# Squares summed after a trip through DRAM, scales spread as rows, and one pair of attention heads taken earlier

## The chip, the cores and the metric

The kernel runs on one core of a Trainium2 chip. The metric is the device time of one execution in microseconds (us). Instruction durations come from the hardware profile of one execution. The five engines each run their own instruction stream in order: PE (matrix multiplies and the transposes made with them), DVE (vector), ACT (scalar), POOL (GpSimd) and SP, which here only issues DMA transfers.

## The reference, cut to what matters

The program is one decoder layer on 512 tokens with 2048 channels. The part that the change touches is the normalisation of queries and keys (per head of 64 channels), the norm of the input, and the LayerNorm of the convolution branch:

```python
h = _rms_norm(x, norm1_g[l])
proj = h @ w_in[l]
aq, ak, av, bu, bg, cq, ck, cv = jnp.split(proj, splits, axis=-1)
aq = _rms_norm(aq.reshape(B, S, A_HEADS, HEAD_DIM), a_q_g[l])
ak = _rms_norm(ak.reshape(B, S, A_HEADS, HEAD_DIM), a_k_g[l])
out_a = _dilated_mixture(aq, ak, av).reshape(B, S, A_WIDTH)
out_b = _conformer_conv(bu, bg, conv_w[l], conv_b[l], conv_ln_g[l], conv_ln_b[l])
cq = _rms_norm(cq.reshape(B, S, C_Q_HEADS, HEAD_DIM), c_q_g[l])
ck = _rms_norm(ck.reshape(B, S, C_KV_HEADS, HEAD_DIM), c_k_g[l])
out_c, _ = _band_attention(cq, ck, cv, C_WINDOW - 1, sinks=c_sinks[l])
mix = jnp.concatenate([out_a, out_b, out_c], axis=-1)
x = x + mix @ w_out[l]
h2 = _rms_norm(x, norm2_g[l])
x = x + (jax.nn.silu(h2 @ w_gate[l]) * (h2 @ w_up[l])) @ w_down[l]
```

`_rms_norm` divides by the root of the mean square over the last axis; A has 8 query heads and three dilated patterns, C has 16 query heads on 2 key heads, B is a gated convolution with 31 taps and a LayerNorm over 512 channels.

## The kernel before, in words

Activations lie with channels on the 128 partitions and the 512 tokens along the row. The input projection is 30 column tiles of 128 channels, taken in the order of the table `PROJ`: value tiles first, then the convolution's (`bu`, `bg`), then C's key tile `ck`, C's eight query tiles `cq0` to `cq7`, and A's key and query tiles `ak0` to `ak3`, `aq0` to `aq3`. A tile holds two heads of 64 channels. Each tile is 16 steps of three matmuls (`mm3`, L318 to L321: the high part of the weights by the high and the low part of the activations, and the low part by the high one), 48 in all.

The output projection follows in two halves. Each takes eight rows of mixed channels in the order of `ROWS`: the first half the eight C rows, the second the A and B rows. After it comes the feed-forward part, from some 605 us to the end, which the change does not touch.

What stands where in each engine's stream is written by hand. A calendar (`Ticks`) is advanced one tick after each six matmuls of an input projection (eight ticks for a tile) and after each twelve of the output projection, and `ticks.after(n, fn)` has `fn` issue its instructions n ticks on. Nothing is measured at run time: a function issues at its tick, and if its data is late, its engine waits there with all that stands behind it.

At the end of a projected query or key tile, `head_scales` (L568) makes the scale of each token and head. ACT copies the tile out of PSUM (`raw`, L571); SQ = 3 ticks later PE transposes the four 128x128 blocks into a PSUM bank (`flip`, L576), so that tokens lie on partitions; ACT squares them (L581); DVE sums each head's 64 squares (a reduce of 128x512 and an addition, L586 to L588); POOL raises the 8 sums of each partition to the power -1/2 (L593). For a query tile (`do_q`) the raw values are also cast into a high part (L609, ACT) and a low part (L614, DVE), and four SP transfers copy halves of them into place (L616, L617). The query's scale is applied later, inside the exponentials of its attention. `"q at"` and `"k at"` are the ticks from which attention heads may use a tile.

For a key tile (`do_k`) the scales must lie along the row, beside the raw values: ACT widens the 8 columns to 512 (`widen`, L630), PE transposes that in four blocks (L637), DVE multiplies (L643), SP copies the halves into the other 64 partitions (L649), ACT and DVE make the high and low parts (L655, L660). The input norm's scale `r1` and the LayerNorm's scale `lrs` are spread in the same way by `spread` (L372), four transposes each (L376). The LayerNorm's scale then multiplies the four convolution tiles `y` on DVE (L560), ACT applies SiLU (L562), and the tiles become rows b0 to b3 of the second half.

The convolution's taps (L521) are 120 DVE instructions set between all of this up to 412 us. The weights of the projections are loaded by SP (L265), cast by ACT (`wh`, L297 and L277) and split by DVE (`wl`, L301 and L278). The attention of a head pair issues scores, exponentials (ACT, L811, with POOL's normalisation L822), transposes on PE (L855) and the weighing of values on PE (L879 and L880, with low parts `a2pl` made on DVE, L866).

Of the kernel before, what the change touches and what calls it, by code (L numbers as in the profile page):

```python
# [15 lines left out]
P = 128  # L16
T = 512
# [24 lines left out]

C_TICKS = (1, 6, 2, 2, 2, 2, 4, 1, 5)
# [4 lines left out]
        "bg2 cq2 cq7 ak2 cq4 cq6 bu3 bg3 ak0 aq0 ak1 aq1 aq2 ak3 aq3").split()  # L48
ROWS = "c0 c3 c1 c5 c2 c7 c4 c6 a0 a1 b2 b1 b0 b3 a2 a3".split()
# [80 lines left out]
def kernel(ctx: ExitStack, tc: tile.TileContext, xT, wi, wo, wgu, wd, cst_in, outT):  # L130
# [241 lines left out]
    def spread(src4, name, b=None):  # L372

        b = bank(name) if b is None else b
        for i in range(NT):
            nc.tensor.transpose(b[:, i * P:(i + 1) * P], src4[:, i:i + 1].to_broadcast([P, P]), ident)  # L376
        return b

# [117 lines left out]

    def spread_r1():
        b = spread(r1, "r1s")
        nc.scalar.copy(r1b, b)
# [57 lines left out]
    def ln_out(mix):  # L557
        b = spread(ln["r"], "lrs")
        for j in range(NB):
            nc.vector.tensor_mul(yconv[j], yconv[j], b)  # L560
        for j in range(NB):
            nc.scalar.activation(yconv[j], yconv[j], AF.Silu, bias=col(C_LB + j), scale=col(C_LG + j))  # L562
            mix[f"b{j}"] = yconv[j]
        for n, name in enumerate(r for r in ROWS if r[0] == "b"):
            ticks.after(1 + n, split_mix, name)


    def head_scales(b, name, then):  # L568
# [10 lines left out]
        def square(b2):  # L579
            sq = slot(name + "sq")  # L580
            nc.scalar.activation(sq, b2, AF.Square)  # L581
            ticks.after(1, total, sq)

        def total(sq):
            v = cp.tile([P, NT, 2], F32, name=name + "v", tag="hsv", bufs=3)
            nc.vector.tensor_reduce(v.rearrange("p a b -> p (a b)"), sq.rearrange("p (a b) -> p a b", b=HD),  # L586
                                    axis=mybir.AxisListType.X, op=ALU.add)
            nc.vector.tensor_add(v, v, c64[:, :, None].to_broadcast([P, NT, 2]))  # L588
            ticks.after(1, power, v)
# [6 lines left out]
        ticks.after(SQ, flip)  # L596
        return raw

    def do_q(box, b, name):
# [3 lines left out]
        raw = head_scales(b, name, then)  # L603
        box["q at"] = ticks.now + SQ + 4
# [15 lines left out]
    def do_k(box, b, name, gi):  # L620
        def then(r):
            ticks.after(KW, widen, r)

        raw = head_scales(b, name, then)
        box["k at"] = ticks.now + SQ + KW + TD + 10
        both = []

# [1114 lines left out]
```

## Time and profile before

| | before |
|---|---|
| median of 3 runs | 1852.05 us (1851.46 to 1852.13) |
| the profiled execution | 1851.51 us |
| its span in the trace | 1849.7 us |
| time around the span | 1.8 us |
| granted PE clock over the span | 1.000 of full speed |
| PE busy, instructions | 1844.3 us, 8548 |
| POOL busy, instructions | 1083.0 us, 681 |

The profiled execution lies 0.54 us under the median of the runs. A row of the trace's timeline gives start, duration, engine, line of the program, operation, output<-inputs, shapes and a count of merged equal instructions; durations of matmuls overlap, so the distance of two starts tells what one costs. A row of a line or tile view gives min/median/max in ns and the first and last start in us. A row of the waits gives the total, the number and the longest of the waits of one kind.

### The profile page before, as it was taken

What the parts mean: (1) busy time and instruction counts of PE and PEld (TensorE: products, weight loads), DVE (VectorE), ACT (ScalarE), POOL (GpSimd) and SP (SyncE); (2) the same over time, 40 slices, a digit from 0 to 9 for tenths busy, and PEclk for the clock granted to TensorE, in tenths of its full rate; (3) what the DMA queues carried; (4) which work ended last, traced back from release to release, by engine and by line L of the source; (5) the groups of instructions that cost most, each with busy time, mean ns of one, the idle gap of its engine ahead of it and who ended that gap; (6) DMA issues with size and microseconds to landing.
All of it is one profiled execution on the core that took longest, in us unless ns stands there. A gap on an engine that the chain in (4) does not pass through costs nothing.

```text
span 1849.7 us, 26751 instructions
## 1 busy us (share of the span) xinstructions
PE 1844.3 (100%) x8548; PEld 1538.4 (83%) x8548; DVE 1533.8 (83%) x2318; ACT 1370.2 (74%) x1956; POOL 1083.0 (59%) x681
## 2 busy tenths in 40 slices
PE   9999999999999999999999999999999999999999
PEld 7888888888888888888888888888888888888888
DVE  7688899997589888898888888888888677779887
ACT  6235555554466788889988889898898987777775
POOL 5013444462153568666685666857667777766786
PEclk9999999999999999999999999999999999999999
DMA  7334333443387459788787887788879786488984
GB/s 263 130 105 115 102 103 95 123 120 120 103 293 272 129 177 295 219 264 272 230 278 227 280 264 234 261 246 264 279 240 371 230 298 222 164 281 284 306 234 125
DMA packets 318556, 398.50 MB, mean 215 GB/s; under 512 B 80976, under 2 KB 210128, under 8 KB 318416
## 3 DMA queue, kind: packets, MB, share of 16 engines
q1 hardware_dynamic: 318272, 396.79, 66.9%
q8 instruction: 68, 1.11, 0.2%
q14 instruction: 72, 0.59, 0.1%
q10 hardware_dynamic: 144, 0.01, 0.0%
HBM read 308.90 MB, written 80.22 MB: 210 GB/s over the span
## 4 chain that ended last, share of the span: by engine, by line
PE 99%; ACT 0%; DVE 0%; DMA 0%; issue 0%; SPq 0%; ACTq 0%; DVEq 0%
PE out L1391 62%; PE out L1283 6%; PE o L321 3%; PE o L319 3%; PE o L320 3%; PE cq L319 2%; PE cq L320 2%; PE cq L321 2%; PE in L320 1%; PE aq L319 1%; PE ak L319 1%; PE ak L321 1%; PE aq L321 1%; PE bu L320 1%; PE ak L320 1%; PE bu L321 1%
## 5 line engine op out<-in xcount | busy, mean ns | idle before, releaser
L1391 PE MATMUL out<-wh,h 128*128 128x512 f32 x2464 | 609.0, 389 | 0.1
L1391 PEld LDWEIGHTS out<-wh,h 128*128 128x128 f32 x2464 | 462.3, 188 | 96.7 <-issue 0.5
L1391 PE MATMUL out<-wl,h 128*128 128x512 f32 x1232 | 329.3, 389 | 0.0
L1391 PEld LDWEIGHTS out<-wl,h 128*128 128x128 f32 x1232 | 231.2, 188 | 48.1
L1391 PE MATMUL out<-wh,a 128*128 128x512 f32 x896 | 221.3, 389 | 0.0
L1391 PEld LDWEIGHTS out<-wh,a 128*128 128x128 f32 x896 | 168.2, 188 | 34.9
L1391 PE MATMUL out<-wl,a 128*128 128x512 f32 x448 | 119.7, 389 | 0.0
L1494 DVE TENSOR_TENSOR G<-G,out 128x512 f32<-128x512 f32 x132 | 83.9, 678 | 18.1 <-PE out L1391 18.1
L1391 PEld LDWEIGHTS out<-wl,a 128*128 128x128 f32 x448 | 84.1, 188 | 17.4
L521 DVE SCALAR_TENSOR_TENSOR y<-bu,cst,y 128x511 f32<-128x511 f32 (+14 forms) x120 | 94.5, 788 | 1.4
L277 ACT CAST wh<-w 128x1024 fp32r<-128x1024 f32 (+1 forms) x41 | 42.1, 1031 | 57.4 <-PE o L320 34.6
L1283 PE MATMUL out<-a,wh 128*128 128x512 f32 x330 | 80.1, 391 | 0.0
L297 ACT CAST wh<-w 128x1024 fp32r<-128x1024 f32 x52 | 54.8, 1054 | 32.3 <-PE bg L320 9.2
L301 DVE TENSOR_TENSOR wl<-w,wh 128x1024 fp32r<-128x1024 f32 x52 | 65.3, 1256 | 14.3 <-ACT wh L297 14.0
L1491 DVE TENSOR_TENSOR G<-G,out 128x512 f32<-128x512 f32 x110 | 68.5, 680 | 5.8 <-PE out L1391 5.8
L1283 PEld LDWEIGHTS out<-a,wh 128*128 128x128 f32 x330 | 60.2, 188 | 11.4
L1532 DVE STREAM_TRANSPOSE z<-s 128x256 f32<-128x256 f32 x88 | 60.1, 683 | 3.0
L278 DVE TENSOR_TENSOR wl<-w,wh 128x1024 fp32r<-128x1024 f32 (+1 forms) x41 | 51.7, 1262 | 9.1 <-ACT wh L277 8.9
L319 PE MATMUL o<-mh_c,wh 128*128 128x512 f32 x128 | 51.2, 400 | 0.0
L321 PE MATMUL o<-mh_c,wl 128*128 128x512 f32 x128 | 50.1, 391 | 0.0
L320 PE MATMUL o<-ml_c,wh 128*128 128x512 f32 x128 | 49.9, 390 | 0.0
L1436 DVE TENSOR_TENSOR Y<-Y,out 128x512 f32<-128x512 f32 x48 | 30.8, 685 | 17.6 <-PE out L1391 17.2
(2758 smaller groups left out, 5123.6 us busy)
## 6 DMA issues: line engine op xcount, KB each, us to landing
h<-hd SPq DMA_DIRECT2D x200, 256.0 KB, 5.8
od<-a SPq DMA_DIRECT2D x154, 256.0 KB, 6.6
a<-od SPq DMA_DIRECT2D x154, 256.0 KB, 6.0
w<-in_wi SPq DMA_DIRECT2D x59, 512.0 KB, 3.5
w<-in_wo SPq DMA_DIRECT2D x32, 512.0 KB, 3.4
hd<-h SPq DMA_DIRECT2D x56, 256.0 KB, 5.2
zd<-z SPq DMA_DIRECT2D x44, 256.0 KB, 4.9
x<-in_xT SPq DMA_DIRECT2D x16, 256.0 KB, 7.4
```

The lines of the kernel that those rows point to most:

```text
L278: eng.tensor_sub(lo[:, :n], t[:, :n], hi[:, :n].bitcast(F32))
L297: nc.scalar.copy(hi, t)
L301: nc.vector.tensor_sub(lo, t, hi.bitcast(F32))
L319: nc.tensor.matmul(out, wh, xh, start=start, stop=False)
L320: nc.tensor.matmul(out, wh, xl, start=False, stop=False)
L321: nc.tensor.matmul(out, wl, xh, start=False, stop=stop)
L521: nc.vector.scalar_tensor_tensor(yconv[j][:, i:], hconv[j][:, :T - i], c, yconv[j][:, i:], op0=ALU.mult, op1=ALU.add)
L1283: nc.tensor.matmul(out, lhs[:, s], rhs, start=begin, stop=last and low == flip[0] and x is xs[-1], skip_group_check=True)
L1391: nc.tensor.matmul(to[h], x[:, h * P:(h + 1) * P], v[:, j], start=sub == 0 and h not in started, stop=sub == 1 and n in (len(todo) - 1, le ...
L1491: op(t, t, b)
L1494: nc.vector.tensor_add(t, t, b)
L1532: nc.vector.transpose(to[:, :, h], s[:, cols].rearrange("p (c b) -> p b c", b=8))
```

## The change

The change has four parts.

1. All twelve query tiles and the key tile `ak2` are "folded". ACT squares the raw tile itself; SP writes the squares to DRAM and two ticks later fetches them back with four transfers, each of which puts 32 rows of four partitions' pieces side by side for one block of 128 tokens; four ticks later POOL adds the four pieces of each partition (a 128x256 and a 128x128 addition); three ticks later PE transposes one 128x128 block in place of four; DVE reduces 16 elements for each sum. From the end of a tile to its scale the calendar has 13 ticks (`FOLDED`) where it had 6.
2. Four scales are spread as rows (`all_rows`): those of the keys `ck` and `ak2`, the input norm's `r1` and the LayerNorm's `lrs`. PE makes one transpose, which gives 4 or 8 rows of 128; ACT copies them out, SP writes them to DRAM and reads them back repeated over the partitions. Before, there were four transposes each, and for keys the widening ahead of them.
3. The four multiplications by the LayerNorm's scale go from DVE to POOL.
4. In `PROJ`, `aq2` moves from behind `aq1` to ahead of `ak0`; in `ROWS`, the second half begins with a2 and a0 and ends with a1 and a3, where it began with a0 and a1 and ended with a2 and a3.

```diff
@@ -40,13 +40,19 @@
 SQ, KW, VD, TD, EV = 3, 4, 4, 2, 1
 
 
+ROW_KEYS = ("ck", "ak2")
+FOLD_AT = (2, 4, 3)
+FOLDED = 2 + sum(FOLD_AT) + 2
+ROWS_FROM, ROWS_AT, LN_ROWS_AT = 2, (1, 2, 3), (1, 1, 2)
+
+
 C_TICKS = (1, 6, 2, 2, 2, 2, 4, 1, 5)
 A_TICKS = (0, 7, 2, 1, 3, 1, 3, 1, 2)
 
 
 PROJ = ("av0 av1 av2 av3 bu0 bg0 bu1 bg1 cv ck cq0 cq3 cq1 cq5 bu2 "
-        "bg2 cq2 cq7 ak2 cq4 cq6 bu3 bg3 ak0 aq0 ak1 aq1 aq2 ak3 aq3").split()
-ROWS = "c0 c3 c1 c5 c2 c7 c4 c6 a0 a1 b2 b1 b0 b3 a2 a3".split()
+        "bg2 cq2 cq7 ak2 cq4 cq6 bu3 bg3 aq2 ak0 aq0 ak1 aq1 ak3 aq3").split()
+ROWS = "c0 c3 c1 c5 c2 c7 c4 c6 a2 a0 b2 b1 b0 b3 a1 a3".split()
 
 N_SLOTS = 68
 N_WIDE = 4
@@ -368,13 +374,6 @@
         rows = small(name + "s")
         nc.vector.tensor_reduce(rows, b.rearrange("p (a b) -> p a b", b=P), axis=mybir.AxisListType.X, op=ALU.add)
         return rows
-
-    def spread(src4, name, b=None):
-
-        b = bank(name) if b is None else b
-        for i in range(NT):
-            nc.tensor.transpose(b[:, i * P:(i + 1) * P], src4[:, i:i + 1].to_broadcast([P, P]), ident)
-        return b
 
     def small(name, cols=NT):
         return cp.tile([P, cols], F32, name=name, tag="small", bufs=24)
@@ -494,9 +493,30 @@
                     ticks.tick()
         return b
 
+    def all_rows(out, src, heads, name, waits, then, *args):
+
+        n = NT * heads
+        b = bank(name + "t")
+        nc.tensor.transpose(b[:n, :P], src, ident)
+        rows = cp.tile([2 * NT, P], F32, name=name + "w", tag="rows", bufs=2)
+        nc.scalar.copy(rows[:n], b[:n, :P])
+        d = tc.dram_tile([n, P], F32, name=name)
+
+        def put():
+            nc.sync.dma_start(d, rows[:n])
+            ticks.after(waits[1], back)
+
+        def back():
+            for h in range(heads):
+                part = out if heads == 1 else out[HALF[h]]
+                nc.sync.dma_start(part.rearrange("p (i c) -> p i c", i=NT),
+                                  bass.AP(tensor=d.tensor, offset=d.offset + h * P,
+                                          ap=[[0, P // heads], [heads * P, NT], [1, P]]))
+            ticks.after(waits[2], then, *args)
+        ticks.after(waits[0], put)
+
     def spread_r1():
-        b = spread(r1, "r1s")
-        nc.scalar.copy(r1b, b)
+        all_rows(r1b, r1, 1, "r1d", ROWS_AT, lambda: None)
 
 
     hconv, yconv = {}, {}
@@ -555,9 +575,12 @@
         ln["r"] = token_scale(ln.pop("s"), 512, "lv")[1]
 
     def ln_out(mix):
-        b = spread(ln["r"], "lrs")
+        b = slot("lrs")
+        all_rows(b, ln["r"], 1, "lrd", LN_ROWS_AT, ln_scale, mix, b)
+
+    def ln_scale(mix, b):
         for j in range(NB):
-            nc.vector.tensor_mul(yconv[j], yconv[j], b)
+            nc.gpsimd.tensor_mul(yconv[j], yconv[j], b)
         for j in range(NB):
             nc.scalar.activation(yconv[j], yconv[j], AF.Silu, bias=col(C_LB + j), scale=col(C_LG + j))
             mix[f"b{j}"] = yconv[j]
@@ -565,7 +588,7 @@
             ticks.after(1 + n, split_mix, name)
 
 
-    def head_scales(b, name, then):
+    def head_scales(b, name, folded, then):
 
         raw = slot(name + "raw")
         nc.scalar.copy(raw, b)
@@ -576,14 +599,36 @@
                 nc.tensor.transpose(b2[:, i * P:(i + 1) * P], raw[:, i * P:(i + 1) * P], ident)
             ticks.after(1, square, b2)
 
-        def square(b2):
+        def square(src):
             sq = slot(name + "sq")
-            nc.scalar.activation(sq, b2, AF.Square)
-            ticks.after(1, total, sq)
-
-        def total(sq):
+            nc.scalar.activation(sq, src, AF.Square)
+            ticks.after(1, *((put, sq) if folded else (total, sq, HD)))
+
+        def put(sq):
+            d = tc.dram_tile([P, T], F32, name=name + "sd")
+            nc.sync.dma_start(d, sq)
+            ticks.after(FOLD_AT[0], fetch, d)
+
+        def fetch(d):
+            parts = slot(name + "p")
+            for i in range(NT):
+                nc.sync.dma_start(parts[i * 32:(i + 1) * 32].rearrange("p (s c) -> p s c", s=4),
+                                  bass.AP(tensor=d.tensor, offset=d.offset + i * P, ap=[[4 * T, 32], [T, 4], [1, P]]))
+            ticks.after(FOLD_AT[1], fold, parts)
+
+        def fold(parts):
+            nc.gpsimd.tensor_add(parts[:, :2 * P], parts[:, :2 * P], parts[:, 2 * P:])
+            nc.gpsimd.tensor_add(parts[:, :P], parts[:, :P], parts[:, P:2 * P])
+            ticks.after(FOLD_AT[2], turn, parts)
+
+        def turn(parts):
+            b2 = bank(name + "f")
+            nc.tensor.transpose(b2[:, :P], parts[:, :P], ident)
+            ticks.after(1, total, b2[:, :P], 16)
+
+        def total(sq, n):
             v = cp.tile([P, NT, 2], F32, name=name + "v", tag="hsv", bufs=3)
-            nc.vector.tensor_reduce(v.rearrange("p a b -> p (a b)"), sq.rearrange("p (a b) -> p a b", b=HD),
+            nc.vector.tensor_reduce(v.rearrange("p a b -> p (a b)"), sq.rearrange("p (a b) -> p a b", b=n),
                                     axis=mybir.AxisListType.X, op=ALU.add)
             nc.vector.tensor_add(v, v, c64[:, :, None].to_broadcast([P, NT, 2]))
             ticks.after(1, power, v)
@@ -593,15 +638,18 @@
             nc.gpsimd.tensor_tensor(r, v, nhalf.rearrange("p (a b) -> p a b", b=2), op=ALU.pow)
             then(r)
 
-        ticks.after(SQ, flip)
-        return raw
+        if folded:
+            ticks.after(1, square, raw)
+        else:
+            ticks.after(SQ, flip)
+        return raw, ticks.now + (FOLDED if folded else SQ + 3)
 
     def do_q(box, b, name):
         def then(r):
             box["rq"] = r
 
-        raw = head_scales(b, name, then)
-        box["q at"] = ticks.now + SQ + 4
+        raw, at_r = head_scales(b, name, True, then)
+        box["q at"] = at_r + 1
         q = box["q"] = [slot(f"{name}{h}", F32R) for h in range(2)]
 
         def high():
@@ -619,11 +667,18 @@
 
     def do_k(box, b, name, gi):
         def then(r):
-            ticks.after(KW, widen, r)
-
-        raw = head_scales(b, name, then)
-        box["k at"] = ticks.now + SQ + KW + TD + 10
+            if name in ROW_KEYS:
+                ticks.after(ROWS_FROM, rows_of, r)
+            else:
+                ticks.after(KW, widen, r)
+
+        raw, at_r = head_scales(b, name, name == "ak2", then)
+        box["k at"] = at_r + (ROWS_FROM + sum(ROWS_AT) - 2 if name in ROW_KEYS else KW) + TD + 7
         both = []
+
+        def rows_of(r):
+            wide = slot(name + "wide")
+            all_rows(wide, r.rearrange("p a b -> p (a b)"), 2, name + "d", ROWS_AT, scale, wide)
 
         def widen(r):
             wide = slot(name + "wide")
```

The engines' streams at the places that matter, before and after. The numbers behind a name are those of buffers. PE, at the end of the query tile `cq3`, where `cq0f` holds the turned squares of `cq0` (before) and `ckt` the turned key scales; before:

```order
L319 MATMUL cq_1099<-hh_290,wh_1030 128x512
L320 MATMUL cq_1099<-hl_291,wh_1030 128x512
L321 MATMUL cq_1099<-hh_290,wl_1031 128x512
L576 MATMUL cq0f<-ident,cq0raw 128x128 x4
L637 MATMUL ckt<-ident,ckwide 128x128 x4
L319 MATMUL cq_1099<-hh_311,wh_1072 128x512
```

and after, where the turned block of folded squares comes during the next tile:

```order
L327 MATMUL cq_1207<-hh_290,wl_1128 128x512
L626 MATMUL cq0f<-ident,cq0p 128x128
L325 MATMUL cq_1207<-hh_311,wh_1177 128x512
```

The group of four at `cq0f` has become one, eight ticks further on, and the group at `ckt` is gone from this place (one transpose `ckdt` stands further ahead in its stead). On ACT, between the casts of weights (`wh`), from the copy of `cq0` to the square of `cq3`; before:

```order
L571 COPY cq0raw<-cq_1011 128x512
L609 CAST cq0hi<-cq0raw 128x512
L297 CAST wh_1118<-w_918 128x1024
L630 COPY ckwide<-ckr 128x512
L581 ACTIVATE cq0sq<-cq0f 128x512
L297 CAST wh_1176<-w_952 128x1024
L655 CAST ckh_1201<-ck_1165 128x512
L655 CAST ckh_1203<-ck_1167 128x512
L571 COPY cq3raw<-cq_1099 128x512
```

and after:

```order
L594 COPY cq0raw<-cq_1012 128x512
L502 COPY ckdw<-ckdt 8x128
L604 ACTIVATE cq0sq<-cq0raw 128x512
L657 CAST cq0hi<-cq0raw 128x512
L303 CAST wh_1127<-w_919 128x1024
L303 CAST wh_1177<-w_953 128x1024
L594 COPY cq3raw<-cq_1100 128x512
L710 CAST ckh_1226<-ck_1187 128x512
L710 CAST ckh_1228<-ck_1189 128x512
L604 ACTIVATE cq3sq<-cq3raw 128x512
L657 CAST cq3hi<-cq3raw 128x512
```

The square now follows its copy directly, and the casts of the key's halves (`ckh`), which wait for the key's trip, stand ahead of the square of `cq3`. On SP at the same place; before:

```order
L616 DMA cq_1097<-cq0hi 64x512
L617 DMA cq_1097<-cq0lo 64x512
L616 DMA cq_1098<-cq0hi 64x512
L617 DMA cq_1098<-cq0lo 64x512
L265 DMA w_1154<-in_wi 128x1024
L649 DMA ck_1165<-ck_1165 64x512
L649 DMA ck_1167<-ck_1167 64x512
```

and after, where `ckd` and `cq0sd` are the DRAM copies of the key's scales and of the squares:

```order
L506 DMA ckd<-ckdw 8x128
L609 DMA cq0sd<-cq0sq 128x512
L664 DMA cq_1098<-cq0hi 64x512
L665 DMA cq_1098<-cq0lo 64x512
L664 DMA cq_1099<-cq0hi 64x512
L665 DMA cq_1099<-cq0lo 64x512
L512 DMA ckwide<-ckd 64x4x128 x2
L271 DMA w_1156<-in_wi 128x1024
L615 DMA cq0p<-cq0sd 32x4x128 x4
L704 DMA ck_1187<-ck_1187 64x512
L704 DMA ck_1189<-ck_1189 64x512
L271 DMA w_1208<-in_wi 128x1024
```

Eight transfers stand among the query's copies, the weights' loads and the key's copies; two of the groups read back what an earlier entry of the same queue writes.

## The prediction

> **What bounds the kernel now.** First the page of the profile, with busy times, the granted clock and the chain that ended last; then PE's waits.
>
> ```profile
> PE 1844.3 (100%) x8548; PEld 1538.4 (83%) x8548; DVE 1533.8 (83%) x2318; ACT 1370.2 (74%) x1956; POOL 1083.0 (59%) x681
> ...
> PEclk9999999999999999999999999999999999999999
> ...
> PE 99%; ACT 0%; DVE 0%; DMA 0%; issue 0%; SPq 0%; ACTq 0%; DVEq 0%
> ...
> PE idle L417 <- DVE bones L350: 1.4, 1, 1.4
> PE a2o L880 <- DVE a2pl L866: 0.3, 1, 0.3
> PE in L320 <- DVE wl L278: 0.2, 1, 0.2
> ```
>
> PE is busy for the whole span, at a clock that never falls below nine tenths, and makes up 99% of the last chain. After the start its waits come to 0.5 us. So the time is the sum of what PE issues: an instruction taken from PE is worth its full issue time unless a wait comes in its place, and work added to another engine costs nothing until PE waits for it.
>
> **What the change takes off PE.** How much does a transpose occupy the queue? The timeline of PE at the end of `cq3`, where two groups of four follow each other, then a place with one group of two:
>
> ```profile
> 131.98 0.39 PE L321 MATMUL cq<-hh,wl 128*128 128x512 f32 x1
> ...
> 132.66 0.39 PE L321 MATMUL cq<-hh,wl 128*128 128x512 f32 x1
> 132.89 0.60 PE L576 MATMUL cq0f<-ident,cq0raw 128*128 128x128 f32 x4
> 133.32 0.60 PE L637 MATMUL ckt<-ident,ckwide 128*128 128x128 f32 x4
> 133.68 0.47 PE L319 MATMUL cq<-hh,wh 128*128 128x512 f32 x1
> 133.99 0.39 PE L320 MATMUL cq<-hl,wh 128*128 128x512 f32 x1
> ...
> 361.04 0.39 PE L321 MATMUL ak<-h,wl 128*128 128x512 f32 x1
> 361.27 0.38 PE L855 MATMUL a0t<-ident,a00e 128*128 128x128 f32 x2
> 361.40 0.48 PE L319 MATMUL ak<-hh,wh 128*128 128x512 f32 x1
> 361.72 0.39 PE L320 MATMUL ak<-hl,wh 128*128 128x512 f32 x1
> ```
>
> Durations overlap, so distances of starts count. From 131.98 to 132.66 stand three matmuls: 0.227 us each. From 132.66 to 133.99 stand two matmuls and eight transposes: 1.33 - 2 x 0.227 = 0.876 us, or 0.1095 each. From 361.04 to 361.72 stand two matmuls and two transposes: 0.68 - 0.454 = 0.226, or 0.113 each. Two and eight give the same price, so there is no fixed part that would stay with the one transpose left.
>
> The thirteen folds (twelve query tiles and `ak2`) and the four scales spread as rows (`ck`, `ak2`, r1, LayerNorm) each make one transpose of four: 17 x 3 = 51 fewer, **51 x 0.1095 = 5.6 us**. The transposes of 8 columns and of 4 have no row in this trace; they move 128 columns as the others do, and I take 0.11 for them too (four instructions: free, they would add 0.4 to the gain, at twice the price take 0.4 off).
>
> [...]
>
> **What the fold needs, and what time it has.** A folded tile's turn comes 1 + 1 + 2 + 4 + 3 = 11 ticks after the tile's end, and a tick is six matmuls: 11 x 6 x 0.227 = 15.0 us. Other instructions of PE (scores, transposes, weighing) stand between. Counted in the streams and priced as above, the distance is 16.4 us at `cq0`, 17.3 at `cq3`, 18.1 at `cq1`, 18.9 at `cq5`, 20.1 at `aq2`, some 20.6 at four more C tiles, 22 to 29 at the last three. The steps to fit into it, by rows of the raw copy, the square, the trip of the value tiles through DRAM (`vd`, written and read back), the queries' copies and POOL's additions:
>
> ```profile
> L571 ACT COPY cq0raw<-cq x1: 587/587/587, 127.6 to 127.6; 128x512 f32<-128x512 f32 x1
> ...
> L581 ACT ACTIVATE cq0sq<-cq0f x1: 597/597/597, 133.5 to 133.5; 128x512 f32<-128x512 f32 x1
> ...
> L1020 SPq DMA_DIRECT2D vd<-vt x4: 319/324/331, 55.4 to 57.1; - x4
> ...
> DMA to landing us min/median/max: 2.0/2.8/4.5
> ...
> 128.96 0.53 SPq L616 DMA_DIRECT2D cq<-cq0hi  x1
> 129.63 0.49 SPq L617 DMA_DIRECT2D cq<-cq0lo  x1
> 130.17 0.59 SPq L616 DMA_DIRECT2D cq<-cq0hi  x1
> 130.82 0.59 SPq L617 DMA_DIRECT2D cq<-cq0lo  x1
> 131.50 0.53 SPq L265 DMA_DIRECT2D w<-in_wi  x1
> ...
> L1147 POOL TENSOR_TENSOR ta<-h,h x6: 730/868/1413, 511.5 to 565.6; 128x256 f32<-128x256 f32 x6
> ```
>
> Copy 0.59, square 0.60, issue of the write 0.33, landing 2.8, four fetches at 0.5 each 2.0, landing 2.8, additions 0.87 each (the smaller one no more than that): 10.9 us. In the SP queue the four copies of the query (128.96 to 131.41, 2.5 us) stand between write and fetch, but lie beside the write's landing, for which the fetch waits anyway. With both landings at the 4.5 us of the slowest row, the issues at 0.53 and 0.59 and the additions at 1.41, it is 0.59 + 0.60 + 0.53 + 4.5 + 2.4 + 4.5 + 2.8 = 15.9. The fetch's pieces of 512 bytes have no row; the bounds are those of `vd`, and I take its median, as it also goes to DRAM and back. So each fold has room by itself, and only the first two are near. But ACT's queue at `cq3` now holds the two casts of the key's halves ahead of the square, and those wait for the key's trip:
>
> ```profile
> 137.51 0.62 ACT L655 CAST ckh<-ck 128x512 fp32r<-128x512 f32 x1 [2.45 <-DMA ck<-ck]
> 138.42 0.62 ACT L655 CAST ckh<-ck 128x512 fp32r<-128x512 f32 x1 [0.29 <-DMA ck<-ck]
> 139.44 0.59 ACT L571 COPY cq3raw<-cq 128x512 f32<-128x512 f32 x1 [0.40 <-PE cq L321]
> ```
>
> Before, ACT had already waited there, 2.45 us, with the copy of `cq3` next. Now the key's scales make a trip through DRAM: issue 0.33, landing 2.8, two reads at 0.5, landing 2.8, 6.9 us, in place of one copy of 0.6, and it begins two ticks (2.7 us) sooner, since the four ticks ahead of the widening become two. So the casts start some 3.6 us later, at 141.1, and the square of `cq3` ends at 143.0; the rest of the median chain (10.9 - 1.2 = 9.7) brings the folded block to 152.7. The tile ended at 139.4 and its turn stands at 156.7: 4 us of room. With landings of 4.5 the key is 3.4 us later and the fold 5.0, together 4.4 more than the room. For these tiles and the first C scores I put **0.5 us** of new waits (ends 0 and 4.4; near the median rows, since two late landings must meet).
>
> **The LayerNorm, and the wait that was there.** Before, DVE's queue held four multiplications at 457.6 to 460 us, then the rest of the attention; PE's one wait in the middle is behind them:
>
> ```profile
> L560 DVE TENSOR_TENSOR y<-y,lrs x4: 678/680/689, 457.6 to 459.4; 128x512 f32<-128x512 f32 x4
> ...
> 467.63 0.38 PE L880 MATMUL a2o<-a2pl,av 128*128 128x256 f32 x1 [0.34 <-DVE a2pl L866]
> ...
> L512 POOL TENSOR_TENSOR bu<-bu,bg x4: 1286/1294/1824, 73.8 to 291.0; 128x512 f32<-128x512 f32 x4
> ```
>
> With 4 x 0.68 = 2.7 us off DVE, and a2's second head placed earlier, this low part should be made in time. In the timeline the weight load waits 0.54 us there; I count **0.5 us gained** (ends 0 and 0.54). In return POOL takes 4 x 1.29 = 5.2 us and the scale goes through DRAM (0.33 + 2.8 + 0.5 + 2.8 = 6.4), so the tiles reach ACT some 9 us later (6.4 + 5.2 - 2.7). The first of them is the third row of the second half, which PE reaches, by the count of its stream, some 25 us on, and POOL is idle for most of that stretch (4.15 us busy of 20, below). That cover hides it; without it PE would wait up to 9 us for that row.
>
> DVE loses the reduce of 512 elements for one of 128, at each fold. POOL gains 26 additions of some 0.8 us on average, and 4 multiplications. SP gains 13 x 5 transfers for the folds and 10 for the rows, some 75 x 0.5 = 38 us of a queue whose weight loads wait, 35 times and 179.9 us in all, for a buffer to be split (first row below), so that they can give way. The new order of A's heads changes no count on PE; it moves two of a2's heads ahead, into the stretch in which DVE still has taps:
>
> ```profile
> SPq L265 <- DVE wl L301: 179.9, 35, 10.0
> ...
> 340.00:360.00 20.00, 20.00 (x101) 16.84 (x100) 19.46 (x52) 11.00 (x21) 10.99 (x8) 1.00 0.44 119
> 360.00:380.00 20.00, 20.00 (x105) 16.80 (x104) 19.54 (x48) 11.13 (x20) 10.30 (x8) 1.00 0.32 93
> 380.00:400.00 20.00, 20.00 (x107) 17.05 (x106) 18.98 (x48) 13.71 (x26) 17.86 (x13) 1.00 0.47 144
> 400.00:420.00 20.00, 20.00 (x100) 16.77 (x99) 18.89 (x42) 8.07 (x13) 8.87 (x7) 1.00 0.49 145
> ...
> 440.00:460.00 20.00, 20.00 (x103) 16.80 (x102) 11.87 (x27) 7.36 (x10) 4.15 (x5) 1.00 0.36 119
> ```
>
> The columns of the windows are the stretch's length, then busy time of PE, weight loads, DVE, ACT, POOL. DVE is busy for 76.87 of 80 us there, with only 3.1 free.
>
> **The sum.** 1851.5 (profiled execution) - 5.6 - 0.5 (the old wait) + 0.5 (new waits) = 1845.9. The execution lies 0.5 us under the median of the runs, so **1846.4 us** stands against 1852.05, 0.3% less.
>
> **Rivals.**
> *New waits eat half the gain.* Two places: `cq0`/`cq3` and the key's trip as worked out above (up to 4.4 us), and DVE at 340 to 420 us. For the second: the taps (L521) vary from 0.71 to 1.69 us,
>
> ```profile
> L521 DVE SCALAR_TENSOR_TENSOR y<-bu,cst,y x120: 707/734/1690, 76.7 to 411.6; 128x511 f32<-128x511 f32 x4, 128x510 f32<-128x510 f32 x4, 128x509 f32<-128x509 f32 x4, 128x508 f32<-128x508 f32 x4
> ```
>
> so something holds single ones up. If each of POOL's additions there (four A folds of 1.6 us, 6.4 in all) held DVE for its whole length, the 3.1 us of room would be short by 3.3. Either gives 1846.4 + 2 to 4.4 = **1848.4 to 1850.8**. For it: DVE's load and the two near chains; against it: the median tap stays at 0.734 with POOL half busy. [...]
>
> *The gain is hidden or cheaper.* Transposes would be worth less than 0.0715 us each where they stand between matmuls, and the gain stays within 3.7 us: 1848.4 to **1852**. The two distances above speak against it. [...]
>
> *The fold is too slow (the other side).* The trip costs more than `vd`'s, since it is cut into 512-byte pieces, and PE waits at turn after turn. With the distances above, a chain of 19.1 us eats the whole gain (2.7 + 1.8 + 1.0 + 0.2 at the first four tiles), and from 20.0 us on (3.6 + 2.7 + 1.9 + 1.1 = 9.3) the kernel is slower by 0.2%. The slowest transfers of this size on the page give the price:
>
> ```profile
> x<-in_xT SPq DMA_DIRECT2D x16, 256.0 KB, 7.4
> ```
>
> With 7.4 us for both landings the chain is 15.9 + 2 x 2.9 = 21.7: late by 5.3, 4.4, 3.6, 2.8, 1.6 (`aq2`) and 4 x 1.1, 22.1 us in all, or 1852.05 - 5.6 + 22.1 = **1868.5**. Against it: that row is the start, with sixteen loads in flight at once; at 100 to 500 us the transfers are few.
>
> **Chances and range.** A measurement of this kernel can tell about 0.2% (3.7 us) from no change. Forecast 0.64 (its own range 1845.0 to 1848.3), half the gain lost 0.22, hidden or cheaper 0.05, too slow 0.09. Hence faster 0.64, within 0.2% 0.27, slower 0.09. The lower end has no new wait and some scatter of the runs; the upper end holds the first rival: 1845.0 to 1850.8.
>
> **What would show it.** Right: 51 fewer matmul records; PE's waits under 1 us beyond the start; the turns (`cq0f` to `aq3f`) with nothing ahead of them; `a2pl` gone from the waits. Wrong: a wait of PE for POOL's additions (`cq0p`, `cq3p`), for the key's high parts at the first C scores, for `wl` or exponentials at 340 to 420 us; transfers of `parts` landing later than 4.5 us; taps slower than 0.734 in the median.

## The result, and the profile after

| | before | after |
|---|---|---|
| median | 1851.82 us (6 runs, 1851.46 to 1852.13) | 1865.45 us (6 runs, 1864.02 to 1866.46) |
| the profiled execution | 1851.51 us | 1864.02 us |
| its span | 1849.7 us | 1862.2 us |
| granted PE clock over the span | 1.000 | 0.997 |

The change makes the kernel slower: the ratio is 1.0073, with a 95% interval of 1.0063 to 1.0084. The forecast was 1846.4 us, and its range ends at 1850.8. The profiled execution is the shortest of the six, 1.4 us under their median; the accounts below are of this one. In the names of tiles, `c60s`, `a00s`, `a10s` and `a11s` are scores of attention heads, `c41t` and `a2t` turned exponentials, `aq2f` and `cq6f` turned squares, `ak2dt` and `ak3t` turned key scales, `lnm` the LayerNorm's mean, `mh_a` and `ml_c` high and low parts of mixed rows, and `wl` low parts of weights. The page of the changed kernel, its chain, and then PE's waits (total, times, longest; the line is that of the waiting instruction, then its releaser):

```profile
PE 1844.8 (99%) x8497; PEld 1535.9 (82%) x8497; DVE 1530.0 (82%) x2314; ACT 1368.7 (73%) x1957; POOL 1100.6 (59%) x711
...
PE 80%; DVE 4%; ACT 1%; DMA 0%; issue 0%; POOL 0%; SPq 0%; DVEq 0%; ACTq 0%; POOLq 0%
...
PE aq2f L626 <- POOL aq2p L621: 4.1, 1, 4.1
PE lnm L562 <- DVE part L560: 2.9, 1, 2.9
PE a10s L823 <- DVE a0pl L921: 2.5, 1, 2.5
...
PE o L327 <- DVE wl L307: 0.9, 1, 0.9
PE a00s L823 <- DVE a2pl L921: 0.9, 1, 0.9
PE c60s L821 <- ACT c40e L866: 0.6, 1, 0.6
PE ak3t L692 <- DVE a0pl L921: 0.6, 1, 0.6
```

PE has exactly 51 instructions fewer and yet is as busy as before (1844.8 us against 1844.3), and it now waits. The chain had been PE's for 99% and is so for 80%; the listed shares add up to 85%, since this chain can be followed back only to 262 us. The waits of the list come to some 12.5 us where before they came to 0.5 after the start; all of them lie between 280 and 437 us. The busy time tells of a second loss: 5.6 us of transposes have gone and something has put 6 us back. The timeline of PE behind the first wait, and the windows of 2 us over it (length, then busy time of PE, weight loads, DVE, ACT and POOL, granted clock, DMA):

```profile
324.19 0.33 PE L626 MATMUL aq2f<-ident,aq2p 128*128 128x128 f32 x1 [4.10 <-POOL aq2p L621]
...
325.06 0.42 PE L325 MATMUL aq<-hh,wh 128*128 128x512 f32 x1
325.30 0.61 PE L326 MATMUL aq<-hl,wh 128*128 128x512 f32 x1
325.70 0.63 PE L327 MATMUL aq<-hh,wl 128*128 128x512 f32 x1
...
324.00:326.00 2.00, 1.80 (x7) 1.46 (x8) 1.37 (x5) 0.00 (x0) 0.14 (x1) 0.83 0.42 131
326.00:328.00 2.00, 2.00 (x8) 1.68 (x7) 0.50 (x1) 0.59 (x1) 0.06 (x1) 0.50 0.00 0
328.00:330.00 2.00, 2.00 (x13) 1.68 (x12) 0.00 (x0) 0.19 (x1) 2.00 (x2) 0.82 0.00 0
330.00:332.00 2.00, 2.00 (x11) 1.65 (x11) 1.58 (x6) 0.40 (x1) 1.56 (x2) 1.00 0.00 0
```

The starts go from 0.24 us apart to 0.40, while the granted clock is 0.50 and PE is busy throughout. From the windows' clocks, (1 - 0.83 + 1 - 0.50 + 1 - 0.82) x 2 = 1.7 us are lost behind this wait. The same is seen behind a10s and lnm (clock 0.50 from 393.6 to 397.0 us and from 438.0 to 441.4 us), 5.1 us in all.

Where the time went, by stretches. For each pair of neighbouring PE instructions the median distance of starts for that pair of shapes in the same trace is taken; what a pair takes beyond it is lost, to waits and to the slow clock together:

| stretch, us of each trace | lost before | lost after | what stands there |
|---|---|---|---|
| 260 to 300 | 0.4 | 1.4 | c60s |
| 300 to 340 | 0.8 | 6.4 | aq2f and the slow clock |
| 340 to 380 | 0.9 | 2.0 | a00s |
| 380 to 420 | 0.9 | 7.1 | a10s and the slow clock, wl, ak3t |
| 420 to 460 | 0.9 | 5.5 | lnm and the slow clock |
| 460 to 500 | 1.5 | 0.5 | a2o, which is gone |

From 100 to 620 us that is 8.4 before and 25.9 after, 17.5 us more; over the whole span it is 10.0 and 27.9, 17.9 us more. With 5.6 gained that leaves 12.3 net, and the spans differ by 12.5.

### The profile page after: what moved, and what is told of

It is laid out like the page before. It is cut to its first block, busy times and chain, and to the rows that moved or that the text cites. A ratio compares the mean times of both kernels' runs of the same rounds, so it can differ in the third digit from the quotient of the medians.

```text
span 1862.2 us, 26829 instructions
## 1 busy us (share of the span) xinstructions
PE 1844.8 (99%) x8497; PEld 1535.9 (82%) x8497; DVE 1530.0 (82%) x2314; ACT 1368.7 (73%) x1957; POOL 1100.6 (59%) x711
## 4 chain that ended last, share of the span: by engine, by line
PE 80%; DVE 4%; ACT 1%; DMA 0%; issue 0%; POOL 0%; SPq 0%; DVEq 0%; ACTq 0%; POOLq 0%
PE out L1446 61%; PE out L1338 6%; PE o L327 3%; PE o L326 3%; PE o L325 3%; DVE y L541 1%; PE aq L327 0%; PE aq L326 0%; PE aq L325 0%; DVE wl L307 0%; PE ak L327 0%; PE ak L325 0%; PE ak L326 0%; DVE wl L284 0%; DMA w<-in_wi 0%
## 5 line engine op out<-in xcount | busy, mean ns | idle before, releaser
L1446 PEld LDWEIGHTS out<-wl,a 128*128 128x128 f32 x448 | 84.1, 188 | 17.5
L307 DVE TENSOR_TENSOR wl<-w,wh 128x1024 fp32r<-128x1024 f32 x52 | 65.4, 1260 | 10.4 <-ACT wh L303 10.2
L1491 DVE TENSOR_TENSOR Y<-Y,out 128x512 f32<-128x512 f32 x48 | 30.8, 683 | 17.9 <-PE out L1446 17.9
```

The source lines that it names most:

```text
L307: nc.vector.tensor_sub(lo, t, hi.bitcast(F32))
L1446: nc.tensor.matmul(to[h], x[:, h * P:(h + 1) * P], v[:, j], start=sub == 0 and h not in started, stop=sub == 1 and n in (len(todo) - 1, le ...
```

## The experiments

Three explanations were open at first: the new order of A's heads (O), the folds' trips (F), and any shift of a calendar without slack (S). The first four kernels undo and do the parts one at a time.

**The old order.** The two tables as before, all else changed.

```diff
-        "bg2 cq2 cq7 ak2 cq4 cq6 bu3 bg3 aq2 ak0 aq0 ak1 aq1 ak3 aq3").split()
-ROWS = "c0 c3 c1 c5 c2 c7 c4 c6 a2 a0 b2 b1 b0 b3 a1 a3".split()
+        "bg2 cq2 cq7 ak2 cq4 cq6 bu3 bg3 ak0 aq0 ak1 aq1 aq2 ak3 aq3").split()
+ROWS = "c0 c3 c1 c5 c2 c7 c4 c6 a0 a1 b2 b1 b0 b3 a2 a3".split()
```

> The change with both tables, PROJ and ROWS, as before; folds, rows and the LayerNorm on POOL stay. Theory O (the new order of A's heads puts more work on DVE while taps are left, and PE's waits at aq2f, a10s, ak3t and lnm follow from that): 1845.5 to 1849 us, all of these waits gone. Theory F (the folds' trips and POOL's additions are late at the A tiles in any order): 1858 us or more, with waits of PE at the turns of aq0 to aq3.

Measured: 1856.36 us, ratio 1.0024 (1.0014 to 1.0033). The waits at aq2f, a10s and lnm are gone, that at ak3t is longer, others stand beside it, and behind the first of these the clock is slow again (0.83 over 510 to 520 us):

```profile
PE o L325 <- ACT mh_a L1066: 2.0, 1, 2.0
...
PE a11s L823 <- issue: 1.4, 1, 1.4
PE ak3t L692 <- DVE a1pl L921: 1.2, 1, 1.2
```

So the order costs 9 us of the 13.6, and without it the rest is still 4.6 us slower than before. Neither expectation fits.

**The order alone**, on the kernel before (the two tables of the change, nothing else).

```diff
-ROWS = "c0 c3 c1 c5 c2 c7 c4 c6 a0 a1 b2 b1 b0 b3 a2 a3".split()
+ROWS = "c0 c3 c1 c5 c2 c7 c4 c6 a2 a0 b2 b1 b0 b3 a1 a3".split()
```

> Before with the two tables PROJ and ROWS of the change; no fold, no rows, the LayerNorm on DVE. Theory O: 1858 to 1864 us, waits at 380 to 440 us as in the changed kernel. Theory F: 1850 to 1853 us.

Measured: 1860.30 us, ratio 1.0044 (1.0027 to 1.0060). The time is in theory O's range: 8.6 us from two tables, with no PE instruction added. The waits are not those of the changed kernel, though: only lnm is among them, while aq2f, a10s, a00s, `wl` and ak3t do not wait here.

```profile
PE lnm L568 <- DVE part L566: 3.6, 1, 3.6
PE o L326 <- POOL ml_c L1072: 1.8, 2, 1.2
```

**The folds alone** (old order, four-transpose spreads, LayerNorm on DVE).

```diff
-ROW_KEYS = ("ck", "ak2")
+ROW_KEYS = ()
...
-            nc.gpsimd.tensor_mul(yconv[j], yconv[j], b)
+            nc.vector.tensor_mul(yconv[j], yconv[j], b)
```

> Before with the thirteen folds alone: old order, scales spread by four transposes, the LayerNorm on DVE. 39 transposes fewer are 4.3 us. Theory O: 1847 to 1849 us. Theory F: 1856 us or more.

Measured: 1859.54 us, ratio 1.0041 (1.0026 to 1.0056): F's side, but not F's mechanism. One turn waits (`cq6f`, 1.7 us, for POOL); the longest others (mh_a 2.0, a11s 1.4, ak3t 1.2 us) are the late A rows of the run with the old order.

**The rows alone** (old order, no fold).

```diff
-        raw, at_r = head_scales(b, name, True, then)
+        raw, at_r = head_scales(b, name, False, then)
```

> Before with the scales spread as rows and the LayerNorm's multiplications on POOL: old order, no fold. 12 transposes fewer are 1.3 us, and the wait at a2o (0.5 us) goes. Both theories: 1849.5 to 1851 us. A time above 1853 would say that the rows' trips make waits of their own.

Measured: 1860.66 us, ratio 1.0047 (1.0032 to 1.0062), far above what both theories gave: here the rows make waits of their own. POOL is late twice, and at the longer one the clock is slow (0.86 over 320 to 330 us, 0.80 over 330 to 340):

```profile
PE c41t L991 <- POOL c61e L984: 3.7, 1, 3.7
PE ak2dt L500 <- POOL ak2r L638: 2.5, 1, 2.5
```

With C's queries and `ak2` folded as well (the next run) these waits do not appear. Parts that cost 8.6, 7.8 and 8.9 us alone make 13.6 together: the costs are waits, and a wait depends on what else stands in the queue. That speaks for S, and asks which queue.

**C folds only, old order.** A's four queries not folded.

```diff
-        raw, at_r = head_scales(b, name, True, then)
+        raw, at_r = head_scales(b, name, name[0] == "c", then)
```

> Old order of both tables; folds for the C queries and ak2 only (A's four queries as before, with their scales seven ticks earlier); rows and the LayerNorm on POOL stay. 39 transposes fewer are 4.3 us, the a2o wait goes (0.5). Theory A (the folded A queries come so late that the last A row and the bank of a1pl are late): the waits at mh_a (2.0), a11s (1.4) and ak3t (1.2) of the run with the old order go, and with them the slow clock at 510 us: 1847 to 1849.5 us. Theory S (any shift of this calendar makes waits of this size somewhere): 1853 us or more.

Measured: 1851.23 us, ratio 0.9999 (0.9989 to 1.0008). The waits at mh_a, a11s and ak3t and the slow clock are gone (1.00 from 500 to 520 us), as theory A says, but the time lies above its range: the 4.3 us still do not show.

```profile
PE o L325 <- ACT a31e L866: 1.7, 1, 1.7
...
PE a0o L935 <- DVE a0pl L921: 0.7, 1, 0.7
PE c60s L821 <- ACT c40e L866: 0.6, 1, 0.6
```

**C folds only, new order**: the same edit on the changed kernel.

> The changed kernel with A's four queries not folded, all else as changed. Theory O (the new order loads DVE at 340 to 440 us): the wait at aq2f goes (4.1 us and some 1.7 us of slow clock behind it, less 1.3 for 12 transposes), the waits at a10s and lnm stay: 1858 to 1861 us. Theory A: these waits go too, 1848 to 1851 us.

Measured: 1860.05 us, ratio 1.0044 (1.0029 to 1.0059), in theory O's range, with lnm at 3.6 us. But a10s, which O had staying, does not wait, nor do a00s, `wl` and ak3t, and `ml_c` waits 1.7 us as with the order alone. The wait at aq2f is gone with its fold; one of 2.9 us has come at `a2t`, for POOL's `a20e`, and whether it is the same lateness is not shown.

```profile
PE lnm L562 <- DVE part L560: 3.6, 1, 3.6
PE a2t L910 <- POOL a20e L877: 2.9, 1, 2.9
PE o L326 <- POOL ml_c L1067: 1.7, 2, 1.2
```

Four of these kernels differ only in the order and in A's four folds; all have C's folds, `ak2`'s fold and the rows:

| | A's queries as before | A's queries folded |
|---|---|---|
| old order | 1851.23 us | 1856.36 us |
| new order | 1860.05 us | 1865.45 us (the change) |

The order costs 8.8 us in one column and 9.1 in the other, A's folds 5.1 in one row and 5.4 in the other, so the two costs add to within 0.3 us, though the waits that make them up differ. What is left, with 39 transposes fewer, is 0.6 us under the kernel before, which its interval cannot tell from no change.

**The wait filled.** Is the slow spacing made by the wait?

```diff
+            for _ in range(18 if name == "aq2" else 0):
+                nc.tensor.matmul(b2, h_hi[10][:, :P], h_hi[10], start=True, stop=True)
             nc.tensor.transpose(b2[:, :P], parts[:, :P], ident)
```

> The changed kernel with 18 matmuls of 512 columns, whose results are overwritten, ahead of the turn of aq2 (18 x 0.227 = 4.1 us, the length of the wait there). If PE's slow spacing after the wait (0.43 us for 0.227) comes from the wait itself, it goes, and the kernel gains some 1.5 to 1.8 us: 1863.5 to 1864. If it comes from something else in the stretch, no gain, or a loss of up to 4 us if the wait isn't what the matmuls lie in: 1865 to 1869.5.

Measured: 1863.70 us (1863.41 to 1863.78), 1.75 below the change's median and inside the first range. Its profiled span is only 0.3 us shorter: the 18 matmuls end 0.7 us later than the wait did, and a00s waits 0.6 us more. What the trace shows is plainer than the time. PE behind the same place:

```profile
324.86 0.33 PE L628 MATMUL aq2f<-ident,aq2p 128*128 128x128 f32 x1
324.95 0.47 PE L325 MATMUL aq<-hh,wh 128*128 128x512 f32 x1
325.26 0.39 PE L326 MATMUL aq<-hl,wh 128*128 128x512 f32 x1
325.49 0.40 PE L327 MATMUL aq<-hh,wl 128*128 128x512 f32 x1
...
318.00:340.00 22.00, 22.00 (x109) 18.02 (x108) 18.72 (x40) 11.66 (x22) 15.16 (x12) 1.00 0.32 103
```

PE has work until the additions are done, the clock is 1.00, the spacing 0.23. So here the idle time of the wait makes the slow clock. In the changed kernel the clock is 0.50 from 325.3 to 328.7 us, and half of these 3.4 us is the 1.7 us seen above. The clock falls behind waits of 2.0 to 2.9 us as well; the last section has when.

**Fewer taps.** DVE relieved by 10 us between 330 and 400 us; the kernel leaves 14 of the 120 taps out.

```diff
+        if j == 3 and 14 <= i < 28:
+            return
         w = TAPS - 1 - i
```

> The changed kernel without 14 of the 120 taps (14 to 27 of the last channel group), that is, 10 us less for DVE between 330 and 400 us. Theory O (DVE's load makes the waits at a10s, ak3t, wl and lnm): these go, 6.9 us and two slow stretches of 1.7: 1854 to 1858 us; the wait at aq2f stays. If they come from the order of POOL or ACT: 1862 us or more.

Measured: 1859.14 us, ratio 1.0037 (1.0024 to 1.0049), just above O's range. The waits at a10s and a00s are gone, which shows DVE's load as their cause, and wl falls to 0.3 us. Lnm and ak3t, which O had going, stay, as does aq2f:

```profile
PE aq2f L628 <- POOL aq2p L623: 4.1, 1, 4.1
PE lnm L564 <- DVE part L562: 3.0, 1, 3.0
...
PE ak3t L694 <- DVE a0pl L923: 0.9, 1, 0.9
```

**The memset.** What does lnm wait for? DVE's timeline of the changed kernel ahead of it, and PE's row:

```profile
431.77 0.69 DVE L555 TENSOR_TENSOR lnl<-lns,lnh 128x512 fp32r<-128x512 f32 x1 [0.74 <-ACT lnh L554]
...
435.78 0.69 DVE L921 TENSOR_TENSOR a1pl<-a1t,a1ph 128x512 fp32r<-128x512 f32 x1
436.44 0.17 DVE L560 MEMSET part<- 128x128 f32 x1
...
436.75 0.47 PE L562 MATMUL lnm<-lnh,part 128*128 128x512 f32 x1 [2.92 <-DVE part L560]
```

The sum of the channels is ready at 432.5; PE waits from 433.8 for a constant of 0.17 us, behind 4 us of other work. In the kernel before the same two rows read

```profile
423.01 0.17 DVE L540 MEMSET part<- 128x128 f32 x1
...
423.45 0.39 PE L542 MATMUL lnm<-lnh,part 128*128 128x512 f32 x1
```

so the memset had stood in the same place and was done 0.3 us ahead of PE. In the changed kernel PE comes here 10.4 us later than before (433.8 against 423.45), but the memset is done 13.4 us later, and the margin of 0.3 us does not cover the difference. Written earlier:

```diff
+        part = ln["part"] = slot("part", F32R)
+        nc.vector.memset(part[:, :P].bitcast(F32), 1.0 / 512)
         nc.vector.tensor_add(s, yconv[0], yconv[1])
```

> The changed kernel with only the constant of the LayerNorm's mean written earlier, ahead of the channel sum. If the wait of 2.9 us at lnm is for this memset alone (it stands in DVE's queue behind 4 us of other work, while the sum itself is ready before PE comes), the wait and the slow clock behind it (1.7 us) go: 1860.5 to 1861.5 us. If the lateness of DVE as such is what PE meets there, it waits at the next thing: 1863.5 us or more.

Measured: 1860.22 us, ratio 1.0043 (1.0028 to 1.0059): 5.2 us in the medians for one moved memset, and the clock behind it is 1.00. The profiled spans differ by 3.7 us, as the profiled execution of the change lies 1.4 us under its median. The clock over the span is still 0.997, as in the changed kernel: by its rounding 4.6 us or more are lost to the slow clock, where the waits at aq2f and a10s lost 3.4 there, so the slow time is longer here.

**aq2's additions.** Was the trip late, or POOL? The fetch of `aq2p`, POOL's timeline, and the DVE rows that the normalisation of `c41e` and `c61e` waited for (it needs all scores of c61s, which PE had made by 305.7):

```profile
L615 SPq DMA_DIRECT2D aq2p<-aq2sd x4: 586/590/597, 310.8 to 312.7; - x4
...
DMA to landing us min/median/max: 2.2/2.6/2.9
...
318.57 1.43 POOL L984 TENSOR_TENSOR c41e<-c41e,c41d 128x512 f32<-128x512 f32 x1 [4.62 <-DVE c41d L981]
319.96 2.02 POOL L984 TENSOR_TENSOR c61e<-c61e,c41d 128x512 f32<-128x512 f32 x1
321.93 1.16 POOL L620 TENSOR_TENSOR aq2p<-aq2p 128x256 f32<-128x256 f32 x1
323.17 0.97 POOL L621 TENSOR_TENSOR aq2p<-aq2p 128x128 f32<-128x128 f32 x1
...
306.93 1.38 DVE L662 TENSOR_TENSOR aq2lo<-aq2raw,aq2hi 128x512 fp32r<-128x512 f32 x1
...
310.62 1.29 DVE L737 TENSOR_TENSOR av<-av2s,av 128x256 fp32r<-128x256 f32 x2
...
312.44 0.41 DVE L840 COPY_PREDICATED c61s<-mask_c,c61s 128x256 f32<-128x256 int32 x1
```

The squares were back by 315.6 us (312.7 + 2.9) and lay there for 6 us. POOL idled for 4.6 us, then worked off two normalisations that stand ahead of the additions; those were late because DVE had handled the scores late. In the new order it makes `aq2`'s low part and its values (2.7 us) ahead of the last mask of c61s. Now that mask is at 312.44; before, with the scores only one us earlier, its row was

```profile
305.87 0.41 DVE L785 COPY_PREDICATED c61s<-mask_c,c61s 128x256 f32<-128x256 int32 x1
```

so the scores are handled 6.6 us later. The order alone does not do this: with it the mask is at 306.2, in the old order with the folds at 309.1, and only with both at 312.4. Two ticks sooner, the additions stand ahead of the normalisations:

```diff
-            ticks.after(FOLD_AT[1], fold, parts)
+            ticks.after(FOLD_AT[1] - 2 * (name == "aq2"), fold, parts)
...
-            ticks.after(FOLD_AT[2], turn, parts)
+            ticks.after(FOLD_AT[2] + 2 * (name == "aq2"), turn, parts)
```

> The changed kernel with POOL's two additions for aq2 two ticks sooner, so that they stand ahead of the normalisation of c41e and c61e in POOL's queue, not behind it; the turn stays at its tick. Theory Q (the squares were back in time, and the additions were late only by their place in POOL's queue): the wait of 4.1 us at aq2f and the slow clock behind it go, less a new wait of up to 1.9 us at c41t for c61e, which POOL still finishes at 322 us: 1859.5 to 1862 us. Theory T (the trip through DRAM is late): no gain, 1864.5 us or more.

Measured: 1861.04 us, ratio 1.0048 (1.0035 to 1.0062), as theory Q: the wait at aq2f is gone, a wait of 0.5 us at c41t comes in its place, and a00s waits 1.9 us for 0.9.

```profile
315.45 0.74 POOL L620 TENSOR_TENSOR aq2p<-aq2p 128x256 f32<-128x256 f32 x1 [1.43 <-PE c40o L1021]
316.27 0.46 POOL L621 TENSOR_TENSOR aq2p<-aq2p 128x128 f32<-128x128 f32 x1
...
322.33 0.33 PE L991 MATMUL c41t<-ident,c61e 128*128 128x128 f32 x1 [0.53 <-POOL c61e L984]
```

**Both repairs**, the two edits above together.

> The changed kernel with both small moves: the additions of aq2 two ticks sooner and the constant of the mean written ahead of the channel sum. If the two waits are separate, their gains add (4 to 6 and 5.2 us): 1854.5 to 1856.5 us, with the waits at a10s, a00s and wl left. If what PE wins at aq2f is lost at a10s or lnm (DVE sets the pace): 1859 us or more.

Measured: 1855.62 us, ratio 1.0022 (1.0012 to 1.0031). The gains add (4.4 + 5.2 = 9.6; measured 9.8). The longest waits left are DVE's, a10s (2.5) and a00s (2.0).

**A version that beats both?** Back to the C folds in the old order, whose longest wait is at 483 us. There ACT stood idle for 3.9 us at 465 to 469 us, until the first of the tiles that POOL multiplies after the scale's trip. So the LayerNorm as before, and the memset early:

```diff
-        all_rows(b, ln["r"], 1, "lrd", LN_ROWS_AT, ln_scale, mix, b)
+        ln_scale(mix, spread(ln["r"], "lrs"))
...
-            nc.gpsimd.tensor_mul(yconv[j], yconv[j], b)
+            nc.vector.tensor_mul(yconv[j], yconv[j], b)
```

> The run with C folds in the old order, with the LayerNorm's scale spread by four transposes again and multiplied on DVE, and the constant of the mean (a memset of 128x128) written ahead of the channel sum instead of just ahead of its matmul. Theory L (the wait of 1.7 us at 483 us comes from the LayerNorm's trip and POOL's multiplications, which hold ACT): that wait goes, some 0.3 us for three transposes and up to 0.5 at a2o come back: 1849.5 to 1850.5 us. If that wait has another cause: 1851 us or more.

Measured: 1850.24 us, ratio 0.9992 (0.9983 to 1.0000); the wait at 483 us is gone: theory L. To see what holds back the rest of the 3.9 us of its 36 transposes, the same 14 taps were left out of it, and, as a control, of the kernel before:

> The kernel of the run before it without 14 of the 120 taps (14 to 27 of the last channel group), 10 us less for DVE between 330 and 400 us. Theory D (from 340 us on DVE sets the pace, so that what PE saves ahead of it turns into waits): with DVE lighter the 36 transposes' 3.9 us show in full: 1847.5 to 1848.5 us. If PE is held by something else: the time of the run before it, within 0.5 us.

> The kernel before without the same 14 taps, the control for the run before it. PE is never late there, so DVE's work can be left out without a gain: 1851 to 1852 us by all theories. Below 1850 DVE would have bounded the kernel before as well.

Measured: 1848.98 us with the folds, 1851.68 without. Before, DVE's load cost nothing; with less work on PE it costs 1.3 us, of which the wait at a0o, gone here, was 0.7. Theory D is right in kind, but the time stays above its range: of the 3.9 us 2.7 show. The last wait, at c60s, belongs to the last C pair, which starts later by its folded query:

```diff
-        raw, at_r = head_scales(b, name, name[0] == "c", then)
+        raw, at_r = head_scales(b, name, name[0] == "c" and name != "cq6", then)
```

> The C folds in the old order with the LayerNorm as before, and cq6, the last C query, not folded. Three transposes come back (0.3 us). If the waits at c60s (0.8 us) and a0o (0.9 us) come from the last C pair's start, seven ticks later with its query folded: they go, 1848.5 to 1849.5 us. If not: 1850.3 to 1851 us.

Measured: 1849.89 us, ratio 0.9990 (0.9981 to 0.9999), 0.1% under the kernel before, at the edge of what the interval can tell. The time lies between the two expectations: the wait at c60s is gone, that at a0o (0.7 us) stays; from its neighbour of 1850.24 the time cannot be told apart.

## Why the prediction was wrong, point by point

- **51 transposes, 5.6 us.** Right: 51 records fewer, and the account above closes to 0.2 us with this price.
- **"So each fold has room by itself", with 0.5 us for new waits.** This step failed. It put the fold's own durations and landings against the distance to its turn. At the fold that waits the landings held: the fetch of `aq2p` landed after 2.2 to 2.9 us. That of `cq0p` took 4.8 to 5.7, beyond the bound of 4.5, and its additions ended 0.4 us ahead of the turn, without a wait. But from the copy of `aq2` to the end of its additions 23.2 us passed, where the chain was put at 10.9 and at most 15.9. What it left out was the place in POOL's queue, behind two normalisations for which DVE had handled the scores 6.6 us late. The prediction asked what stands behind a waiting instruction, and for the additions not what stands ahead. DVE's load was summed over a stretch, and never followed at c61s.
- **A's heads start seven ticks later.** The fold moves the scale from 6 ticks behind the tile to 13, and the heads that use it with it. The prediction had no term for that. A's four folds cost 5.1 us in the old order and 5.4 in the new one, after the 1.3 us that their transposes give; in the old order no turn of theirs makes PE wait, and mh_a, a11s and ak3t do. Whether the later start or the additions on POOL makes these waits, no run separates.
- **The new order "changes no count on PE".** True, and it cost 8.6 to 9.1 us, against a term of nothing. The first rival named DVE's 3.1 free us of 80 and allowed 3.3 us at most, with a chance of 0.22. Its mechanism is shown in part: a10s and a00s go when DVE has less work. But a00s, a10s and `wl` (0.9 + 2.5 + 0.9 = 4.3 us) wait only where the new order and A's folds come together, and ak3t wherever A's queries are folded; the order alone makes the wait at lnm. A move of two heads' DVE work into a stretch that is 96% full should have been a term of the sum.
- **A wait was priced at its own length.** In the profiled execution the slow clock behind three waits cost 1.7 us each, 5.1 of the 12.5 us. No term had it; the trace of before has no such wait.
- **The LayerNorm.** The wait at a2o went, as forecast. The tiles did not delay PE in the new order; with C's folds in the old order they did (1.7 us), so the cover of 25 us was not there. The memset was not seen: its margin before was 0.3 us, and the prediction looked at waits that exist, not at margins that are small.
- **"The fold is too slow"** was the rival on the slower side. That the kernel came out slower, and only 3.1 us under that rival's time, is luck: no turn of the changed kernel waited for a transfer.
- **What stays open.** C's folds and the rows together gain 0.6 us at the medians, where their 39 transposes and the wait at a2o would give 4.8; the waits found there (1.7 us at 483 us, a0o, c60s, lnm) come to 3.3 of these 4.2 us. Which part of DVE's lateness at a10s comes from the heads and which from POOL's work beside it was not tried; one tap of 1.73 us stands there, but the median tap is 0.734 as before, and no run shows that an addition on POOL holds DVE for its whole length, from which the first rival's 3.3 us were worked out.

## What to carry to other kernels

When the bounding engine is relieved in a schedule written out by hand, list for each place where it takes another engine's result how early that result was: where the other engine falls behind by more than that margin, a wait comes, and the gain ends there. Read the queue ahead of an added instruction on its own engine, as well as its inputs. Ask what starts later because a result is due later. Make constants long before they are used.

## What the runs showed of the hardware that was not expected

After a wait of PE, its granted clock can fall to 0.50. In the changed kernel it is 0.50 from 325.31 to 328.72 us, from 393.57 to 396.98 and from 437.95 to 441.36, behind aq2f, a10s and lnm: 3.41 us each time, which costs 1.7 us on top of the wait. The clock of 0.83 over 10 us behind mh_a in the old order, behind lnm with the order alone and with fewer taps, and behind a10s with the wait filled comes to the same 1.7 us. At c41t with the rows alone it is 0.86 and then 0.80, which comes to 3.4 us, or 6.8 us at 0.50. With the memset early, and with the additions sooner, two waits of 2.5 us or more are left and the clock over the span is 0.997, where runs with two such waits (C folds in the new order, wait filled, fewer taps) have 0.998: there the slow time is longer as well.

The slow clock came behind waits of 4.1, 2.9, 2.5 and, with the old order, 2.0 us. It did not come behind 1.7 us (C folds, old order, 1.00 over 480 to 500 us), 2.0 us at a00s (both repairs, 1.00 over 340 to 360 us) or 2.5 us at ak2dt (rows alone, 1.00 over 240 to 260 us). A wait of 2.0 us lost 1.7 us more to the clock in one run and nothing in another, and so did one of 2.5 us: the length alone does not decide.

In the trace of the changed kernel the three stretches of half clock, 3.413 us each in its records, begin 20.0 and 13.0 of these lengths apart. Cut into stretches of this length that begin with them, between 20 and 1840 us, it has this much idle time of PE:

| stretch of the changed kernel | wait in it | PE idle in it, us | clock in the next |
|---|---|---|---|
| 318.5 to 321.9 us | aq2f, 4.1 us, first part | 1.80 | 1.00 |
| 321.9 to 325.3 | aq2f, second part | 2.30 | 0.50 |
| 390.2 to 393.6 | a10s, 2.5 us, most of it | 1.81 | 0.50 |
| 434.5 to 437.9 | lnm, 2.9 us, most of it | 2.22 | 0.50 |
| every other | | 0.86 or less | 1.00 |

In this one trace half clock follows the three stretches with the most idle time. Whether it is the place of a wait among such stretches that decides was not tried: no run shifts a wait on purpose.
